# Another order of the expert passes in the two mixture-of-experts stages

## The chip, the cores and the metric

One core of one Trainium2 chip runs the whole kernel. The metric is the device time of one execution in microseconds (us). The times below are those of whole executions; the rows come from one profiled execution of the same program.

## What is computed

Two blocks of two layers each act on 256 tokens of width 1024, all in fp32. The first block alternates a token mixer with a mixture of experts (MoE): in each of its two layers a router gives every token two of 16 experts, out of one group of four, and an expert is a gated pair of products. The second block (attention and a dense MLP) is not touched by the change. Of the reference, this is the part at issue:

```python
logits = h2 @ router_w; scores = sigmoid(logits)
...
def run_block(args):
    tok, g, e = args
    xb = h2[tok]
    y = (silu(xb @ w1[e]) * (xb @ w3[e])) @ w2[e]
    return y * g[:, None]
```

Each expert has w1 and w3 (1024 x 512) and w2 (512 x 1024), 2 MB (of 1,048,576 bytes) each in fp32: 6 MB an expert, 96 MB a layer, and every expert's weights are read once per layer.

## The kernel before

**Ranks and passes.** The router counts the tokens of each expert and ranks the experts by that count, rank 0 having the most. Lists of ranks, not of experts, are fixed in the program: `PASSES` (line 23) holds seven passes. A pass of one expert uses all 128 columns of TensorE's array for up to 128 tokens; a pass of two gives each expert 64 columns, a pass of four gives each 32. Which ranks share a pass sets how many tokens a rank may have (`CAPS`, line 25); tokens beyond that go through `overflow` (line 797), a branch that stands between the last two passes and that is passed over here. `GROUPS` (line 24) names the passes, by their place in the order, that are prepared together.

**Loads.** Weights come in loads of 1 MB each, half of a matrix, on SP's queue in exactly the order of `sources()`: the up loads of pass p, then the down loads (w2) of pass p-1. A load of rank r needs that rank's expert number in a register of SP (line 889). The loads land in nine buffers in turn (`KINDS["wide"]`), so load k+9 can be issued only when the matmuls of load k are done. Each layer has 96 loads; they are numbered 1 to 96 here.

```python
def sources():
    up = lambda p: [(A[w], r, j) for w in ("w1", "w3") for j in range(2) for r in PASSES[p]]
    down = lambda p: [(A["w2"], r, j) for j in range(2) for r in PASSES[p]]
    for p in range(NP + 1):
        yield from up(p) if p < NP else ()
        yield from down(p - 1) if p else ()
```

**Matmuls.** `tiles` (line 954) takes the loads of one matrix half of a pass together, here called a group: one load in a pass of one expert, two or four otherwise. Its 4 products for each expert are issued in turn over the experts, whose columns of the array work side by side, and the first matmul of a group waits until all its loads have landed (line 963). A pass has four groups up (`up_`: two of w1, two of w3) and two groups down (`down`).

**Order of the work on TensorE.** `prep(g)` (line 916) gathers the tokens of the passes of one group of `GROUPS` with one-hot matmuls (lines 933 to 944). `up_(p)` ends with SiLU, a product and four transposes (line 976). `combine` (line 993) adds two finished passes into xT (lines 1000, 1002). The loop over p runs up_(p), down(p-1), after every second pass combine, and prep of the next group, two passes ahead:

```python
for p in range(NP + 1):
    if p < NP:
        at[p] = up_(p, pr[p])
    if p:
        todo.append((pr[p - 1][1], down(p - 1, at.pop(p - 1))))
        if len(todo) == 2 or p == NP:
            combine(todo)
...
    if groups and GROUPS[groups[0]][0] == p + 2:
        pr.update(prep(groups.pop(0)))
    if p == NP - 2:
        fetch(KINDS["wide"][0])
```

The Tile framework may move single instructions of an engine past each other where no data forbids it; the queue of loads keeps the order above.

Of the kernel before, what the change touches and what calls it, by code (L numbers as in the profile page):

```python
# [19 lines left out]
S = 256  # L20
D = 1024
NE = 16
PASSES = [[8, 9, 10, 11], [0], [2, 3], [4, 5], [1], [6, 7], [12, 13, 14, 15]]
GROUPS = [[0, 1], [2, 3], [4, 5], [6]]
CAPS = [128 // len(p) for _, p in sorted((r, p) for p in PASSES for r in p)]
ALPHA = 4.0 ** 0.25
# [175 lines left out]
def body(tc, A, out, co, po):  # L202
# [3 lines left out]
    with ExitStack() as ctx:  # L206
# [654 lines left out]
        def moe(l):  # L861
# [30 lines left out]
# [7 lines that stand above are left out]
            def fetch(n):  # L899

                while len(ahead) < n:
                    w, r, j = next(todo_w, (None, 0, 0))
                    if w is None:
                        break
                    ahead.append((load(w[l][expert(r), j].rearrange("o p a n -> p (o a n)"), None, 2048), landing[0]))

            def taken(p):
                n = len(PASSES[p])
                fetch(n)
                return [ahead.pop(0) for _ in range(n)]  # L910

            NP = len(PASSES)
            todo_w = sources()
            wide = lambda p: 128 // len(PASSES[p])

# [701 lines left out]
```

## Time and profile before

| | |
|---|---|
| median of 3 runs | 1955.6 us (1955.56 to 1958.34) |
| the profiled execution's own time | 1955.22 us |
| its span, first to last instruction | 1953.4 us |
| mean granted TensorE clock | 0.959 of 2.4 GHz |
| first MoE layer: first load issued, last group of matmuls begun | 202.7 us, 457.55 us |
| second MoE layer: first load issued, last group of matmuls begun | 606.1 us, 858.35 us |

The time of an execution lies 1.8 us over its span. The two MoE layers take a quarter of the span between them. Busy time is a share of the whole span, over stages with different limits; the rows of a stage tell more.

### The profile page before, as it was taken

To read this page: it belongs to the slowest core of one execution; us is meant where nothing else is said; L and a number is where in the kernel's file an instruction comes from. 1 tells how busy PE (TensorE), PEld (TensorE's weight loads), DVE (VectorE), ACT (ScalarE), POOL (GpSimd) and SP (SyncE) were. 2 spreads that over 40 slices of the span, in tenths; PEclk is the share of its full clock that TensorE was granted. 3 is DMA by queue.
4 is the path that set the end of the run, shared out by engine and by line. 5 is a ranking of instruction groups with operands and counts; after the bars stand their busy time and mean duration, and the time that the engine had idled before them with its cause. 6 is when DMAs were issued, how large, how long until landed. Compare 5 with 4: busy or idle time off the path is not lost. (4 is left out here: it accounts for less than half of the span.)

```text
span 1953.4 us, 29087 instructions
## 1 busy us (share of the span) xinstructions
PE 1758.2 (90%) x11198; PEld 1256.4 (64%) x11198; DVE 1078.6 (55%) x2298; ACT 741.2 (38%) x1461; POOL 70.7 (4%) x88
## 2 busy tenths in 40 slices
PE   5999689967897799689999999999999999989997
PEld 4866234414783344237655779888888786669996
DVE  4987212104654112048778367678855767666665
ACT  3556100003642000124767355232323656544443
POOL 0000000000200000000010001000000200010000
PEclk8999899978998999889999999999999999989999
DMA  9685999997649999984100675555543220245551
GB/s 378 242 285 193 382 413 419 371 381 311 242 164 369 417 423 380 386 343 156 35 21 33 218 253 188 176 172 187 188 129 130 97 93 22 76 153 182 183 184 44
DMA packets 94361, 440.46 MB, mean 225 GB/s; under 512 B 10240, under 2 KB 10368, under 8 KB 69376
## 3 DMA queue, kind: packets, MB, share of 16 engines
q1 hardware_dynamic: 94208, 438.44, 60.0%
q8 instruction: 93, 1.52, 0.3%
q14 instruction: 60, 0.49, 0.1%
HBM read 437.35 MB, written 1.05 MB: 224 GB/s over the span
## 5 line engine op out<-in xcount | busy, mean ns | idle before, releaser
L332 ACT CAST wh<-raw 128x1024 fp32r<-128x1024 f32 (+1 forms) x258 | 261.4, 1016 | 281.8 <-PE psL L346 209.8
L325 DVE TENSOR_TENSOR wl<-raw,wh 128x1024 fp32r<-128x1024 f32 (+1 forms) x258 | 305.3, 1185 | 97.8 <-ACT wh L332 97.4
L959 PE MATMUL psab<-raw,xg 128*32 128x512 f32 (+2 forms) x1024 | 226.2, 705 | 76.1 <-DMA raw<-w 62.8
L344 PE MATMUL psL<-h,wh 128*128 128x256 f32 (+1 forms) x800 | 258.4, 323 | 7.6 <-ACT h L340 7.6
L345 PE MATMUL psL<-h,wl 128*128 128x256 f32 (+1 forms) x800 | 257.8, 323 | 4.0 <-DVE wl L325 3.9
L346 PE MATMUL psL<-h,wh 128*128 128x256 f32 (+1 forms) x800 | 256.4, 321 | 0.0
L959 PEld LDWEIGHTS psab<-raw,xg 128*32 128x32 f32 (+2 forms) x1024 | 73.9, 147 | 221.7 <-issue 193.7
L344 PE MATMUL psL<-gh,wh 128*128 128x256 f32 (+1 forms) x576 | 185.1, 322 | 0.0
L345 PE MATMUL psL<-gh,wl 128*128 128x256 f32 (+1 forms) x576 | 184.6, 321 | 0.0
L344 PEld LDWEIGHTS psL<-h,wh 128*128 128x128 f32 x800 | 154.2, 193 | 23.4 <-ACT h L340 8.3
L973 DVE SCALAR_TENSOR_TENSOR sa<-sa,gs,psab 128x512 f32<-128x512 f32 x14 | 10.5, 747 | 282.5 <-PE psab L959 282.5
L345 PEld LDWEIGHTS psL<-h,wl 128*128 128x128 f32 x800 | 154.2, 193 | 18.5 <-DVE wl L325 5.1
L346 PEld LDWEIGHTS psL<-h,wh 128*128 128x128 f32 x800 | 153.9, 193 | 14.2 <-issue 4.2
L959 PE MATMUL psY<-raw,at 128*32 128x512 f32 (+2 forms) x512 | 113.1, 611 | 9.3 <-DMA raw<-w 8.4
L346 PE MATMUL psL<-o,wh 128*128 128x256 f32 (+1 forms) x384 | 119.3, 311 | 0.3
L344 PEld LDWEIGHTS psL<-gh,wh 128*128 128x128 f32 x576 | 109.5, 190 | 14.5 <-issue 5.8
L345 PEld LDWEIGHTS psL<-gh,wl 128*128 128x128 f32 x576 | 109.5, 190 | 11.1 <-issue 3.7
L340 ACT CAST yh<-psY 128x512 fp32r<-128x512 f32 x28 | 16.4, 586 | 245.5 <-PE psY L959 245.5
L346 PE MATMUL psL<-gl,wh 128*128 128x256 f32 (+1 forms) x288 | 91.9, 319 | 0.0
L1525 ACT ACTIVATE t<-psL 128x256 f32<-128x256 f32 (+1 forms) x72 | 32.8, 456 | 139.1 <-PE psL L346 139.1
L1123 DVE SCALAR_TENSOR_TENSOR xT<-psL,mod2T,xT 128x256 f32<-128x256 f32 x80 | 38.6, 483 | 84.2 <-PE psL L346 84.0
L344 PE MATMUL psL<-hh,wh 128*128 128x256 f32 x256 | 77.8, 305 | 7.0 <-ACT hh L518 5.5
(449 smaller groups left out, 3340.9 us busy)
## 6 DMA issues: line engine op xcount, KB each, us to landing
raw<-w SPq DMA_DIRECT2D x192, 1024.0 KB, 11.7
raw<-fc SPq DMA_DIRECT2D x144, 512.0 KB, 3.5
raw<-mod_w SPq DMA_DIRECT2D x80, 512.0 KB, 6.6
raw<-w_mod SPq DMA_DIRECT2D x80, 512.0 KB, 3.9
raw<-wo SPq DMA_DIRECT2D x24, 512.0 KB, 4.7
raw<-wi SPq DMA_DIRECT2D x18, 512.0 KB, 3.3
raw<-ev_in SPq DMA_DIRECT2D x16, 512.0 KB, 7.4
raw<-mod_w SPq DMA_DIRECT2D x8, 1024.0 KB, 10.3
```

What stands on the lines that cost most here:

```text
L325: eng.tensor_sub(o, a, hi)
L332: SC.copy(hi[:, :w], raw[:, :w])
L340: SC.copy(hi, src)
L344: T.matmul(o, lhsT=wh, rhs=xh, start=start, stop=False)
L345: T.matmul(o, lhsT=wl, rhs=xh, start=False, stop=False)
L346: T.matmul(o, lhsT=wh, rhs=xl, start=False, stop=stop)
L959: r = T.matmul(o[w * i:w * i + w, :], lhsT=x[:, w * i:w * i + w], rhs=loads[i][0][:, c:c + 512], start=first, stop=last)
L973: V.scalar_tensor_tensor(sa, sa, gs, ob, op0=OP.mult, op1=OP.mult)
L1123: V.scalar_tensor_tensor(src2[s][:, n, :], o[:, s * S:s * S + S], mod2T[l][:, g, s, n:n + 1], src2[s][:, n, :], op0=OP.mult, op1=OP.add)
L1525: SC.activation(t[:, a:b], o[:, a:b], AF.Relu)
```

## The change

One line: the order in which the seven passes run. The lists within the passes stay, and with them the capacities; `GROUPS` stays and so joins other passes: prep(0) still serves ranks 0 and 8 to 11, prep(1) now serves ranks 1, 2, 3, and prep(2) ranks 4 to 7. The last two passes stay where they are.

```diff
-PASSES = [[8, 9, 10, 11], [0], [2, 3], [4, 5], [1], [6, 7], [12, 13, 14, 15]]
+PASSES = [[0], [8, 9, 10, 11], [1], [2, 3], [4, 5], [6, 7], [12, 13, 14, 15]]
 GROUPS = [[0, 1], [2, 3], [4, 5], [6]]
```

Loads and groups in the order of SP's queue, "4 x 1" being four groups of one load; u is up, d is down:

| | before | after |
|---|---|---|
| loads 1 to 20 | u 4 x 4, u 4 x 1 | u 4 x 1, u 4 x 4 |
| loads 21 to 38 | d 2 x 4, u 4 x 2, d 2 x 1 | d 2 x 1, u 4 x 1, d 2 x 4, u 2 x 2 (of 4 x 2) |
| loads 39 to 58 | u 4 x 2, d 2 x 2, u 4 x 1, d 2 x 2 | u 2 x 2, d 2 x 1, u 4 x 2, d 2 x 2, u 1 x 2 (of 4 x 2) |
| loads 59 to 68 | u 4 x 2, d 2 x 1 | u 3 x 2, d 2 x 2 |
| loads 69 to 96 | u 4 x 4, d 2 x 2, d 2 x 4 | the same |

## Rows read from the trace of the kernel before

**Rows 1.** The page: busy engines, and 40 slices of DMA rates.
```profile
PE 1758.2 (90%) x11198; PEld 1256.4 (64%) x11198; DVE 1078.6 (55%) x2298; ACT 741.2 (38%) x1461; POOL 70.7 (4%) x88
...
GB/s 378 242 285 193 382 413 419 371 381 311 242 164 369 417 423 380 386 343 156 35 21 33 218 253 188 176 172 187 188 129 130 97 93 22 76 153 182 183 184 44
```

**Rows 2.** TensorE's timeline, end of the first MoE layer: start, duration, work, [idle].
```profile
457.55 5.34 PE L959 MATMUL psY<-raw,at 128*32 128x512 f32 x26 [1.39 <-DMA raw<-w]
```

**Rows 3.** First layer, stretches: busy by engine, granted clock, DMA share, GB/s.
```profile
270.00:280.00 10.00, 9.03 (x71) 3.15 (x69) 1.69 (x3) 0.60 (x2) 0.00 (x0) 1.00 0.95 369
...
340.00:350.00 10.00, 10.00 (x26) 4.29 (x23) 1.38 (x2) 1.61 (x3) 0.00 (x0) 1.00 1.02 428
370.00:380.00 10.00, 10.00 (x61) 5.27 (x62) 1.01 (x3) 1.00 (x3) 0.00 (x0) 1.00 0.55 203
380.00:390.00 10.00, 10.00 (x43) 3.84 (x40) 1.44 (x2) 0.55 (x1) 0.00 (x0) 1.00 0.96 392
400.00:410.00 10.00, 8.86 (x60) 2.76 (x64) 0.00 (x0) 1.48 (x2) 0.00 (x0) 0.67 0.55 209
```

**Rows 4.** The same stretches of the second layer.
```profile
680.00:690.00 10.00, 7.17 (x41) 2.40 (x32) 1.38 (x2) 1.17 (x2) 0.00 (x0) 0.83 0.98 392
770.00:780.00 10.00, 10.00 (x70) 6.75 (x71) 2.95 (x8) 0.96 (x2) 0.00 (x0) 1.00 0.58 220
780.00:790.00 10.00, 10.00 (x45) 3.38 (x42) 0.75 (x1) 0.60 (x1) 0.00 (x0) 1.00 0.95 398
800.00:810.00 10.00, 7.06 (x52) 2.14 (x56) 0.00 (x0) 1.47 (x2) 0.00 (x0) 0.70 0.61 235
```

**Rows 5.** SP's queue: loads 68 and 78 issued, each with its time to landing.
```profile
L321 SPq DMA_DIRECT2D raw<-w x1: 333/333/333, 376.5 to 376.5; - x1
...
DMA to landing us min/median/max: 7.4/7.4/7.4
...
L321 SPq DMA_DIRECT2D raw<-w x1: 333/333/333, 407.5 to 407.5; - x1
...
DMA to landing us min/median/max: 4.7/4.7/4.7
```

**Rows 6.** TensorE's timeline, first layer, later: passes of two, combine, the branch.
```profile
308.48 0.68 PE L1000 MATMUL psX<-PT,yh 128*128 128x256 f32 x1
...
318.04 13.95 PE L959 MATMUL psab<-raw,xg 128*64 128x512 f32 x64
...
340.59 14.00 PE L959 MATMUL psab<-raw,xg 128*128 128x512 f32 x32
...
401.14 9.80 PE L959 MATMUL psab<-raw,xg 128*32 128x512 f32 x64 [6.89 <-DVEq L804]
```

**Rows 7.** TensorE's timeline, first layer, passes [8, 9, 10, 11] and [0].
```profile
214.51 0.50 PE L944 MATMUL psX<-rt,P 128*128 128x1 f32 x4
217.00 3.64 PE L959 MATMUL psab<-raw,xg 128*32 128x512 f32 x32 [1.98 <-DMA raw<-w]
226.70 6.54 PE L959 MATMUL psab<-raw,xg 128*32 128x512 f32 x32 [6.07 <-DMA raw<-w]
...
246.24 7.23 PE L959 MATMUL psab<-raw,xg 128*32 128x512 f32 x36 [4.67 <-DMA raw<-w]
253.31 0.60 PE L976 MATMUL psX<-cst,sa 128*128 128x128 f32 x4
...
258.78 12.26 PE L959 MATMUL psab<-raw,xg 128*128 128x512 f32 x28
271.96 0.65 PE L976 MATMUL psX<-cst,sa 128*128 128x128 f32 x4 [0.92 <-DVE sa L973]
```

**Rows 8.** TensorE's timeline, start of the second layer's passes.
```profile
619.26 0.50 PE L944 MATMUL psX<-rt,P 128*128 128x1 f32 x4
619.70 3.64 PE L959 MATMUL psab<-raw,xg 128*32 128x512 f32 x32
629.58 6.49 PE L959 MATMUL psab<-raw,xg 128*32 128x512 f32 x32 [6.24 <-DMA raw<-w]
```

## The prediction

> **What bounds the kernel now.** I read the page first. TensorE is busy for 90% of the span, but in the slices of the two MoE layers (the fifth to the tenth and the thirteenth to the eighteenth) the DMA engines move 370 to 420 GB/s, more than anywhere else [rows 1]. So in these stages the loads are to be looked at, not the busy share. The timeline at the end of a layer says it plainly: the last group starts at 457.55, when its loads land, with TensorE idle before it [rows 2]. What comes after (5.3 us of matmuls, combine, the next norm) hangs on that moment alone, so a change is worth what it moves the landing of load 96 in each layer.
>
> Next I read the layers in stretches of 10 us. Where the queue is full it moves 428 GB/s [rows 3], which is 1,048,576 bytes / 428 GB/s = 2.45 us a load. The reader is to look for stretches with less: there SP held no free buffer. What a stretch lost is 10 x (1 - rate/428). The first layer lost 1.4 at 270, 5.3 and 0.8 at 370 and 380, and 5.1 at 400: 12.6 us [rows 3]. The second lost the same three holes: 0.8 at 680, 4.9 and 0.7 at 770 and 780, 4.5 at 800: 10.9 us [rows 4]. Together 23.5 us of DMA time.
>
> The holes of 370 and 400 are those of loads 68 and 78: each was issued late, at 376.5 and 407.5, and landed 7.4 and 4.7 us later [rows 5]. Both waited for a buffer. In the timeline TensorE works without idle time before load 68: passes of two and the lone pass [1] take 14.0 us each, whether a group is one load or two [rows 6]. A group costs 14.0 / 4 = 3.5 us; at full rate DMA brings one, two or four loads in 2.45, 4.9 or 9.8 us. A lone pass is thus slower than DMA (3.5 against 2.45 a load), the others faster. TensorE waits early, on [8, 9, 10, 11]: 6.07 and 4.67 us shown, a third such wait between them [rows 7]; then it runs late, and nine buffers do not span the lateness.
>
> **The change, step by step.** Its matmuls, loads, bytes and instructions are the same in number; only places change. Loads 69 to 96 come in the same order. The register loads of expert numbers move: four loads of one expert come first and need one number instead of four. That is at most a microsecond or two, and nothing hangs on it, since the first group can't start before prep(0) is done: taken as 0.
>
> *Start.* prep(0) ends at 214.51 + 0.50 = 215.0 [rows 7] and at 619.7 in the second layer [rows 8]. Before, TensorE then waited for four loads, until 217.0. Now load 1 is enough. Four lone groups take 4 x 3.5 = 14.0: to 229.0 and 633.7. Their buffers come back one by one, long before DMA has brought the nine loads that it holds.
>
> *The new hole, at load 14.* Next in the program stand the transposes and prep(1): from 253.31 to 258.78 before, 5.5 us [rows 7], with 0.92 ahead of the transposes for `sa`, as at 271.96 [rows 7], and 0.2 of slack: 6.6. So the first group of [8, 9, 10, 11] starts at 235.6 and takes 3.64, as the group of 217.0 [rows 7]: its four buffers come back at 239.2 (second layer: 643.9), and load 14 is issued 0.1 later. By then the queue is empty: load 13 is due at 217.0 + 9 x 2.45 = 239.05; in the second layer load 8 lands at 629.58 [rows 8] and load 13 at 641.8. A load issued to an empty queue lands after 4.7 to 7.4 us [rows 5]; I take the mean, 6.05. Load 14 lands at 245.35 instead of 241.5, hole 3.85, and at 650.05 instead of 644.25, hole 5.8. Sum 9.7; 7.0 at the shorter end, 12.4 at the longer.
>
> The Trainium skill (DMA: Bandwidth & Descriptors, Anatomy of one DMA) puts a transfer at a fixed 2.0 us plus bytes over 436 GB/s, fitted on another issue path: an estimate of 4.4 us for 1 MB. The row of load 78, 4.7, is near it; that of load 68 is not, as other loads followed at once and shared the engines. By the page the new holes would sum to 6.4 and the time would be 1939.1.
>
> *After load 14.* I count from load 20, which TensorE waits for (260.05 in the first layer: 245.35 + 6 x 2.45). Its group, after a wait, takes 5.5 (7.23 less four records of the next lone group [rows 7]); transposes 1.5 (0.92 and 0.65 [rows 7]), six lone groups 21.0, transposes 1.5, the first down group of four 3.5: 33.0. Load 36 is issued then and lands at 39.05 after load 20; due are 16 x 2.45 = 39.2. No hole, barely; with 6.5 for the first group, as the one at 226.70 had [rows 7], 0.85.
>
> From load 34 (294.35) TensorE has 3.5 left of that pass, combine and prep(2) 9.6 (308.48 to 318.04 [rows 6]), 14.0, 1.5, 7.0, 14.0, 1.5, 7.0, again at most 9.6: it begins up of [6, 7] at 362.0. Load 59's group ends at 369.0; load 68 lands at 375.05, and is due at 245.35 + 54 x 2.45 = 377.65. The hole of load 68 goes: lone pass [1] no longer stands in this stretch.
>
> TensorE ends the pass before the branch at 362.0 + 14.0 + 1.5 + 7.0 = 384.5 and starts again 6.9 later [rows 6], at 391.4; a group of 3.5 to 6.5 us; load 78 lands at 400.95 to 403.95, due 402.15. Hole 0 to 1.8, where there were 5.1. For this and load 36 I take 0.5 a layer, bounds 0 and 2.65. The second layer runs through the same sum from its load 20.
>
> *Sum.* Old holes 23.5, less new ones 9.7, less 1.0: 12.8 us sooner. The profiled execution took 1955.2 (span 1953.4 and 1.8 around it), 0.4 under the median: 1955.2 - 12.8 = 1942.4. Ends: 23.5 - 7.0 - 0 = 16.5 (1938.7), and 23.5 - 12.4 - 5.3 = 5.8 (1949.4).
>
> **Rivals.** *prep(1) is not in the way.* The order on TensorE isn't strictly the program's: four records of the next pass went ahead of the transposes (36 records at 246.24, then 28 [rows 7]). If prep(1) runs in the wait for load 16 instead, the first group of four ends at 229.0 + 1.5 + 3.65 = 234.1, load 14 lands at 240.2, before it is due; in the second layer at 644.9, 0.6 late. Gain 23.5 - 0.6 - 1.0 = 21.9: 1933.3. Against it: prep(1) came before the bulk of the next pass in this trace.
>
> *The hole moves to load 36.* Six lone groups stand in a row there and the margin is 0.15. If TensorE is 6.4 us later a layer at that point than I sum, as two of the six groups at half the clock would make it, the gain is gone: 1955.2; from 4 us on it is mostly gone. For it: groups behind waits took 6.54 and 6.49 instead of 3.64 [rows 7, 8]. Against it: the lone groups behind the wait of 246.24 ran 28 records in 12.26 us, full speed [rows 7].
>
> *Slower: the first lone groups run at 1.2 GHz.* They stand where load 14 depends on them. At 6.5 instead of 3.5, four of them bring load 14 12 us later in each layer: 1942.4 + 24 = 1966.4. It decides from 3.5 + 12.8/8 = 5.1 us a group on. For it: the group at 629.58 took 6.49 [rows 8]. The Trainium skill (TensorE: Matmul & The Clock Gate, HAM oscillation) tells of groups that start cold after each wait for DMA; the rows behind waits agree. Against it: the first group of each layer took 3.64, right behind prep(0) [rows 7, 8], and the lone groups would stand in that very place.
>
> **How the numbers follow.** The forecast (8 to 19 us gained) 0.58; more, through prep(1) or short landings, 0.14; 4 to 8, a part of the margin lost, 0.10; within 3.9 us (0.2%, about what a measurement here can tell from nothing), through load 36, 0.09; slower 0.09. Faster 0.82. The likeliest: 1942.4, own range 1938.7 to 1949.4. For 8 in 10 the range takes in most of the second and third case: 1933 to 1951.
>
> **What would show it.** In the profile after, rates stay at 420 GB/s or more from load 20 to the end of a layer: no stretch near 203 or 220. One new stretch falls short shortly after 239 and 644, by 3 to 6 us. TensorE's first four groups have 8 records each of 3.5 us, start at 215, and prep(1) follows. It waits for loads 16 and 20. The branch ends near 391 instead of 401, and the last group starts near 448 instead of 457.55. The prediction is wrong if the first lone groups take over 5 us, if load 14 is issued much before or after 239, or if the rate breaks in at load 36 or 78.

## The result, and the profile after

| | before | after |
|---|---|---|
| median of 4 runs each | 1956.97 us | 1942.94 us (1940.48 to 1943.91) |
| the profiled execution, its span | 1955.22, 1953.4 us | 1940.48, 1938.7 us |

The ratio of the two is 0.9913 with a 95% interval from 0.9896 to 0.9930: 0.7 to 1.0% faster. Forecast were 1942.4 us and a gain of 12.8; the profiled executions differ by 14.7, the medians by 14.0.

Stretches of the kernel after, first layer and second (columns as in [rows 3]); where they repeat those of [rows 3] and [rows 4], DMA now runs at or near its full rate, and one new place in each layer, two stretches long, does not:

```profile
230.00:240.00 10.00, 9.79 (x88) 6.92 (x92) 3.75 (x16) 1.89 (x4) 0.00 (x0) 1.00 0.59 249
240.00:250.00 10.00, 3.55 (x32) 0.85 (x28) 0.00 (x0) 0.60 (x1) 0.00 (x0) 0.89 0.96 381
...
290.00:300.00 10.00, 9.72 (x77) 3.60 (x70) 1.86 (x4) 1.17 (x2) 0.00 (x0) 1.00 1.01 422
...
370.00:380.00 10.00, 9.05 (x44) 3.15 (x42) 1.44 (x2) 0.00 (x0) 0.00 (x0) 1.00 1.01 424
380.00:390.00 10.00, 3.04 (x18) 1.19 (x18) 1.38 (x2) 2.69 (x5) 0.00 (x0) 0.89 1.01 421
...
400.00:410.00 10.00, 5.49 (x40) 1.38 (x35) 0.00 (x0) 0.60 (x1) 0.00 (x0) 0.84 1.01 426
...
620.00:630.00 10.00, 9.08 (x66) 6.77 (x68) 3.77 (x13) 1.89 (x4) 0.00 (x0) 1.00 0.94 399
630.00:640.00 10.00, 6.02 (x59) 1.56 (x48) 0.57 (x5) 0.60 (x1) 0.00 (x0) 1.00 0.64 251
...
770.00:780.00 10.00, 6.11 (x30) 2.10 (x26) 1.38 (x2) 2.45 (x3) 0.00 (x0) 1.00 1.02 428
...
800.00:810.00 10.00, 5.08 (x32) 1.31 (x32) 0.00 (x0) 0.00 (x0) 0.00 (x0) 0.79 1.02 430
```

Lost at 428 GB/s, reckoned as in the prediction: 4.2 and 1.1 us at 230 and 240, 0.7 and 4.1 at 620 and 630, together 10.1 (forecast for load 14: 9.7). The stretches of 370, 380 and 400, which lost 11.2 us of the first layer before [rows 3], lose 0.3; those of 770 and 800 in the second, which lost 9.4 [rows 4], lose nothing.

TensorE's timeline after, first layer (columns as in [rows 2]). The reader is to see the four lone groups at the front (32 records, eight to a group), without a wait among them; transposes and prep(1) to 235.8; two groups of [8, 9, 10, 11] back to back, whose loads had long landed; then the waits for loads 16 and 20:

```profile
214.95 0.51 PE L944 MATMUL psX<-rt,P 128*128 128x4 f32 x4
215.31 13.98 PE L959 MATMUL psab<-raw,xg 128*128 128x512 f32 x32
230.21 0.66 PE L976 MATMUL psX<-cst,sa 128*128 128x128 f32 x4 [0.92 <-DVE sa L973]
...
235.82 7.07 PE L959 MATMUL psab<-raw,xg 128*32 128x512 f32 x64
249.34 6.29 PE L959 MATMUL psab<-raw,xg 128*32 128x512 f32 x32 [6.45 <-DMA raw<-w]
259.25 6.45 PE L959 MATMUL psab<-raw,xg 128*32 128x512 f32 x32 [3.62 <-DMA raw<-w]
...
389.81 6.02 PE L959 MATMUL psab<-raw,xg 128*32 128x512 f32 x32 [6.96 <-DVEq L804]
...
447.88 3.64 PE L959 MATMUL psY<-raw,at 128*32 128x512 f32 x26 [1.39 <-DMA raw<-w]
```

The last group starts at 447.88, before 457.55 [rows 2]. In the second layer it starts 17 us sooner than the 858.35 of before, but its 26 records take 5.52 us where the same records took 3.64 before; the first line is of the kernel before, the second of the kernel after:

```profile
858.35 3.64 PE L959 MATMUL psY<-raw,at 128*32 128x512 f32 x26 [1.41 <-DMA raw<-w]
...
841.38 5.52 PE L959 MATMUL psY<-raw,at 128*32 128x512 f32 x26 [0.52 <-DMA raw<-w]
```

SP's queue of loads after: load 13 of the first layer, load 14 of both layers, and load 78 of the first.

```profile
L321 SPq DMA_DIRECT2D raw<-w x1: 332/332/332, 229.3 to 229.3; - x1
...
DMA to landing us min/median/max: 8.4/8.4/8.4
...
L321 SPq DMA_DIRECT2D raw<-w x1: 333/333/333, 239.5 to 239.5; - x1
...
DMA to landing us min/median/max: 4.9/4.9/4.9
...
L321 SPq DMA_DIRECT2D raw<-w x1: 333/333/333, 632.6 to 632.6; - x1
...
DMA to landing us min/median/max: 4.7/4.7/4.7
...
L321 SPq DMA_DIRECT2D raw<-w x1: 332/332/332, 395.8 to 395.8; - x1
...
DMA to landing us min/median/max: 7.0/7.0/7.0
```

### The profile page after: what moved, and what is told of

It reads as the page before. It is cut to its first block, busy times and chain, and to the rows that moved or that the text cites. A ratio compares the mean times of both kernels' runs of the same rounds, so it can differ in the third digit from the quotient of the medians.

```text
span 1938.7 us, 29085 instructions
## 1 busy us (share of the span) xinstructions
PE 1757.4 (91%) x11198; PEld 1255.2 (65%) x11198; DVE 1078.4 (56%) x2298; ACT 741.2 (38%) x1461; POOL 69.3 (4%) x88
## 5 line engine op out<-in xcount | busy, mean ns | idle before, releaser
L959 PE MATMUL psab<-raw,xg 128*32 128x512 f32 (+2 forms) x1024 | 220.2, 691 | 60.4 <-DMA raw<-w 46.6
L344 PEld LDWEIGHTS psL<-h,wh 128*128 128x128 f32 x800 | 154.6, 193 | 23.5 <-ACT h L340 8.3
L340 ACT CAST yh<-psY 128x512 fp32r<-128x512 f32 x28 | 16.4, 585 | 273.9 <-PE psY L959 273.9
L1123 DVE SCALAR_TENSOR_TENSOR xT<-psL,mod2T,xT 128x256 f32<-128x256 f32 x80 | 38.7, 483 | 84.2 <-PE psL L346 83.9
L959 PEld LDWEIGHTS psY<-raw,at 128*32 128x32 f32 (+2 forms) x512 | 35.9, 132 | 75.9 <-issue 59.2
## 6 DMA issues: line engine op xcount, KB each, us to landing
raw<-w SPq DMA_DIRECT2D x192, 1024.0 KB, 12.8
```

The lines of the kernel that those rows point to most:

```text
L344: T.matmul(o, lhsT=wh, rhs=xh, start=start, stop=False)
L959: r = T.matmul(o[w * i:w * i + w, :], lhsT=x[:, w * i:w * i + w], rhs=loads[i][0][:, c:c + 512], start=first, stop=last)
L1123: V.scalar_tensor_tensor(src2[s][:, n, :], o[:, s * S:s * S + S], mod2T[l][:, g, s, n:n + 1], src2[s][:, n, :], op0=OP.mult, op1=OP.add)
```

## The experiments

The theory under test: in both layers time is lost only where DMA has no free buffer, so the time follows from the sum of these holes, wherever they stand. A hole is what a stretch moved less than 428 GB/s, put as time. Rivals were that the gain comes from the earlier start (one landed load instead of four), that TensorE's work merely moves, and that early lone passes are good in themselves. Each kernel was timed in five rounds beside the kernel before, whose medians were 1958.69 us with the first four kernels and 1960.86 with the second four; ratios are to those. Medians of different rounds can differ by as much as those of the kernel before do (1956.97, 1958.69, 1960.86), so kernels of different rounds are best compared by their ratios.

**Half of the change: [0] to the front.**

```diff
-PASSES = [[8, 9, 10, 11], [0], [2, 3], [4, 5], [1], [6, 7], [12, 13, 14, 15]]
+PASSES = [[0], [8, 9, 10, 11], [2, 3], [4, 5], [1], [6, 7], [12, 13, 14, 15]]
```

> Half of the change alone: pass [0] goes to the front, pass [1] stays fifth. Theory of the buffers (time is lost only where DMA has no free buffer): the hole near load 14 appears (about 4 us a layer), the one at load 30 (about 2 us) goes, and those at loads 68 and 78 stay, since the lone pass [1] still stands between the passes of two. Net -1 to +3 us against the kernel before: 1954 to 1958. Rival, the early start (the gain comes from beginning each layer on one landed load instead of four): nearly the whole gain, 1941 to 1945.

Measured: 1961.81 us, ratio 1.0015 (1.0003 to 1.0028). The early start alone gains nothing: it is 3.1 us slower by the medians, at the slow end of what was expected (-1 to +3). Stretches of its first layer, columns as before:

```profile
230.00:240.00 10.00, 9.08 (x74) 6.50 (x75) 4.34 (x16) 1.89 (x4) 0.00 (x0) 1.00 0.76 320
240.00:250.00 10.00, 4.89 (x48) 1.29 (x40) 0.00 (x0) 0.60 (x1) 0.00 (x0) 0.85 0.74 294
270.00:280.00 10.00, 10.00 (x39) 3.64 (x39) 1.38 (x2) 1.17 (x2) 0.00 (x0) 1.00 1.01 425
370.00:380.00 10.00, 10.00 (x63) 5.71 (x64) 1.48 (x5) 0.96 (x2) 0.00 (x0) 1.00 0.77 301
...
400.00:410.00 10.00, 7.95 (x52) 2.40 (x56) 0.00 (x0) 1.47 (x2) 0.00 (x0) 0.63 0.53 206
```

The new hole is there (2.5 and 3.1 us), the one at 270 is gone, and those of 370 and 400 stay (3.0 and 5.2 us, where they were 5.3 and 5.1): the new one is paid and little is bought with it. That the early start by itself makes the gain is ruled out.

**The other half: [1] from fifth to third.**

```diff
+PASSES = [[8, 9, 10, 11], [0], [1], [2, 3], [4, 5], [6, 7], [12, 13, 14, 15]]
```

> The other half alone: [8, 9, 10, 11] stays first, pass [1] moves up to third. Theory of the buffers: load 30 stays late (2 us), eight lone groups in a row make a new hole at load 44 (4 to 5 us), load 68 is on time and load 78 late by 1 to 2 instead of 5. About 5.5 us a layer gained: 1942 to 1946. Rival, the early start: no gain, 1953 to 1957.

Measured: 1945.12 us, ratio 0.9937 (0.9915 to 0.9960). Most of the gain is here, perhaps all of it: the interval overlaps that of the change (0.9896 to 0.9930), so it is not shown that moving [0] to the front adds anything to moving [1].

```profile
270.00:280.00 10.00, 9.08 (x73) 2.96 (x72) 1.74 (x3) 0.58 (x1) 0.00 (x0) 1.00 0.90 361
310.00:320.00 10.00, 10.00 (x48) 3.48 (x49) 0.63 (x4) 1.01 (x3) 0.00 (x0) 1.00 0.77 303
370.00:380.00 10.00, 9.05 (x44) 3.06 (x42) 1.44 (x2) 0.60 (x1) 0.00 (x0) 1.00 1.01 424
400.00:410.00 10.00, 3.76 (x36) 1.18 (x32) 0.00 (x0) 0.60 (x1) 0.00 (x0) 0.84 1.00 419
```

The holes of 370 and 400 go when no lone pass stands between the passes of two, the one at 270 stays, and the two lone passes one behind the other open a new one at 310 (2.9 us, load 44; 4 to 5 were expected).

**prep(1) held back into the wait for load 16.** The order of the change, but the matmuls of prep(1) may stand on TensorE only behind the second group of [8, 9, 10, 11]; an order on the same engine, no new wait.

```diff
-            def prep(g):
+            def prep(g, behind=None):
+                def put(r):
+                    if behind:
+                        tc.add_manual_dep(r.ins, behind, nosync, reason="prep in the wait")
...
-            def up_(p, pr):
+            def up_(p, pr, between=None):
...
                 for o in (oa, ob):
+                    if o is ob and between:
+                        between()
...
-                    at[p] = up_(p, pr[p])
+                    at[p] = up_(p, pr[p], (lambda: pr.update(prep(groups.pop(0), last_mm[0]))) if p == 1 else None)
```

> The changed kernel with prep(1) held back on TensorE until the second group of [8, 9, 10, 11], that is into the wait for load 16. Theory of the buffers: load 14 is issued 5 us earlier, its hole (4.2 and 4.7 us) goes, and prep(1) costs nothing where it stands: 8 to 9 us under the changed kernel, 1932 to 1936. Rival (the hole only moves on, to load 36, since TensorE's work is the same in sum): within 2 us of the changed kernel.

Measured: 1933.63 us, ratio 0.9868 (0.9849 to 0.9886), which lies below the interval of the changed kernel: it beats both. Its timeline, first layer (line 937 is prep, line 965 the groups):

```profile
230.43 3.64 PE L965 MATMUL psab<-raw,xg 128*32 128x512 f32 x32
235.19 3.64 PE L965 MATMUL psab<-raw,xg 128*32 128x512 f32 x32 [1.12 <-DMA raw<-w]
238.76 0.50 PE L937 MATMUL psX<-P,th 128*128 128x256 f32 x2
...
242.45 0.41 PE L937 MATMUL psX<-P,tl 128*128 128x256 f32 x2
244.98 3.64 PE L965 MATMUL psab<-raw,xg 128*32 128x512 f32 x32 [0.94 <-DMA raw<-w]
```

and its rates in the first layer, with no hole at load 14 and none that came in its place:

```profile
230.00:240.00 10.00, 8.88 (x78) 3.56 (x78) 0.69 (x1) 0.60 (x1) 0.00 (x0) 1.00 1.01 422
240.00:250.00 10.00, 7.68 (x68) 4.89 (x67) 2.90 (x14) 1.89 (x4) 0.00 (x0) 1.00 1.01 428
290.00:300.00 10.00, 9.89 (x80) 7.61 (x73) 5.96 (x12) 1.76 (x3) 0.00 (x0) 1.00 1.01 424
```

The first group of four now ends at 234.1, the time that the rival of the prediction had worked out for it, and load 14 is issued at 234.1 instead of 239.5. Moving prep(1), 5.5 us long, out of the front of this release was worth 9.3 us by the medians (8.8 by the ratios), that is some 4.5 us a layer: most of its length, and in the wait it cost nothing that these rows show.

**prep(1) one pass later.**

```diff
-                if groups and GROUPS[groups[0]][0] == p + 2:
+                if groups and GROUPS[groups[0]][0] == p + (1 if groups[0] == 1 else 2):
```

> The changed kernel with prep(1) one pass later: after the whole of up of [8, 9, 10, 11] and the down groups of [0]. Theory of the buffers: load 14 is on time, but prep(1) now stands in the row of six lone groups, where the margin of load 36 was near 0: a hole of 4 us at loads 34 to 36 takes the place of the one at load 14. No change against the changed kernel, 1940 to 1945. If the hole at load 14 were only a matter of the place of prep(1) and margins elsewhere were wide, 8 us less.

Measured: 1939.98 us, ratio 0.9906 (0.9887 to 0.9925); the changed kernel had 0.9913 (0.9896 to 0.9930). The hole went from 230 to 290:

```profile
230.00:240.00 10.00, 7.34 (x65) 2.46 (x68) 1.44 (x2) 0.00 (x0) 0.00 (x0) 1.00 1.01 427
280.00:290.00 10.00, 10.00 (x27) 4.03 (x25) 0.75 (x1) 0.60 (x1) 0.00 (x0) 1.00 0.99 408
290.00:300.00 10.00, 9.89 (x82) 4.26 (x81) 2.41 (x4) 1.17 (x2) 0.00 (x0) 1.00 0.88 341
```

0.5 and 2.0 us here, 1.8 in the second layer's stretch of 680 (352 GB/s), so somewhat less than the 4 expected; in time it can't be told from the change. That is the prediction's rival of the hole that moves to load 36, brought about by the edit.

**Eight buffers instead of nine**, in the kernel before, the changed one and the one with prep(1) in the wait; more than nine was not tried.

```diff
-        KINDS = {"long": (11, 1024, 4), "wide": (9, 2048, 0), "short": (6, 1024, 3)}
+        KINDS = {"long": (11, 1024, 4), "wide": (8, 2048, 0), "short": (6, 1024, 3)}
```

> The kernel before with eight buffers of 1 MB instead of nine. Theory of the buffers: each old hole grows (loads 27 to 29 by 2.5 us, load 47 by 2.5, load 67 stays at that of load 68 plus what DMA runs ahead), about 5 us a layer: 8 to 12 us over the kernel before in the same runs. Rival (the lost time is TensorE's own, not DMA's): no change.

> The changed kernel with eight buffers. Theory of the buffers: the hole of load 14 comes one load sooner and is 2.45 us longer, and a new one of 1.6 us opens at load 35: 4.4 us a layer, 7 to 11 us over the changed kernel: 1948 to 1953. It stays faster than the kernel before with nine. Rival: no change.

> prep(1) in the wait for load 16 (now with eight buffers). Theory of the buffers: holes of 1.3 us at load 13 and 1.6 at load 35, 3.2 to 3.8 us a layer: 6 to 8 us over the same kernel with nine buffers, 1939 to 1943, about as fast as the changed kernel with nine.

Measured: 1976.97 us (ratio 1.0094, 1.0070 to 1.0119), 1959.32 (1.0002, 0.9986 to 1.0018) and 1948.31 (0.9944, 0.9926 to 0.9961). Against the same kernels with nine buffers that is 16.1, 16.4 and 14.7 us more: the direction of the theory, in no case the size of the expectation (8 to 12, 7 to 11, 6 to 8). The changed kernel with eight was expected to stay faster than the kernel before with nine; it is no faster. Part of the difference lies ahead of the layers. Each layer begins with loads of the conditioning weights in the same buffers, which I had left out: the first load of an expert is issued at 205.9 in the changed kernel with eight, at 202.1 with nine. And the hole at load 14, now load 13, is 8.1 us long, not 5.3 + 2.45:

```profile
230.00:240.00 10.00, 9.08 (x57) 6.82 (x55) 2.82 (x4) 1.52 (x3) 0.00 (x0) 1.00 0.77 305
240.00:250.00 10.00, 7.10 (x65) 1.99 (x65) 1.52 (x12) 0.97 (x2) 0.00 (x0) 0.97 0.54 203
```

The rest is in further holes: from the first load issued to the last group begun, the two layers together take 11.4, 12.4 and 14.2 us longer with eight buffers than with nine, and the stretches under 428 GB/s account for 11.3, 12.4 and 13.5 of it (table below). In the changed kernel with eight, 2.3 us of it stand at 400 and 420 of the first layer (371 and 385 GB/s), where no hole was expected.

**Another order altogether.**

```diff
+PASSES = [[2, 3], [4, 5], [0], [6, 7], [8, 9, 10, 11], [1], [12, 13, 14, 15]]
```

> A wholly different order with nine buffers and prep where the program puts it: [2, 3], [4, 5], [0], [6, 7], [8, 9, 10, 11], [1], [12, 13, 14, 15]. Each lone pass stands between passes of two or four, so that TensorE never falls far behind. Theory of the buffers: no hole at load 14, one of 2.3 us at load 72: 1932 to 1938, near the kernel with prep(1) in the wait. If what counts is lone passes early, as in the changed kernel, it is slower than that one: 1945 or more.

Measured: 1944.7 us, ratio 0.9922 (0.9901 to 0.9944): as fast as the change, but 6.7 us over the upper end of the expectation. It lost more than summed:

```profile
290.00:300.00 10.00, 10.00 (x57) 4.60 (x57) 1.13 (x5) 1.93 (x4) 0.00 (x0) 1.00 0.84 332
...
370.00:380.00 10.00, 10.00 (x36) 4.08 (x38) 0.75 (x1) 0.60 (x1) 0.00 (x0) 1.00 0.98 375
380.00:390.00 10.00, 6.17 (x56) 1.80 (x56) 2.07 (x3) 2.45 (x3) 0.00 (x0) 1.00 0.87 331
```

A hole of 2.2 us at 290 that I had put at nothing, and 1.2 and 2.3 at 370 and 380 for one of 2.3: 3.4 us more in this layer, and 3.5 in the second, whose stretches of 690, 770 and 780 moved 333, 306 and 397 GB/s. So the miss is again in holes that were held to be just avoided, not in another place. The time by itself stands at the border of the rival (1945 or more); what speaks against it is that no lone pass is among the first two here and the time is that of the change all the same.

## Why the prediction was right

*What sets the end of a layer.* Shown: in both layers of all ten kernels the last group begins within 0.1 us of the landing of load 96. The table has, of each profiled execution, the holes (of both layers, every whole stretch of 10 us under 428 GB/s from 5 us after the first load's issue on), the two layers from first load issued to last group begun, and the median.

| kernel | holes, us | two layers, us | median, us |
|---|---|---|---|
| prep(1) in the wait | 3.3 | 481.9 | 1933.63 |
| prep(1) later | 7.3 | 486.2 | 1939.98 |
| the change | 12.4 | 491.4 | 1942.94 |
| another order altogether | 13.7 | 493.3 | 1944.70 |
| [1] alone moved | 13.6 | 492.6 | 1945.12 |
| prep(1) in the wait, 8 buffers | 16.8 | 496.1 | 1948.31 |
| before | 27.4 | 507.1 | 1956.97 |
| the change, 8 buffers | 24.8 | 503.8 | 1959.32 |
| [0] alone moved | 30.8 | 509.2 | 1961.81 |
| before, 8 buffers | 38.7 | 518.5 | 1976.97 |

Less their holes the layers take 478.4 to 479.8 us in all ten. As the bytes are the same, holes and layers must go together; what the table adds is that no layer's end waited for anything else, and that the medians rise in nearly the same order. That a hole comes from a missing buffer is shown by the issue times: load 14 after the change was issued at 239.5, within 0.1 us of the end of the group that gave its buffer back, when load 13 had landed at 237.7.

*The start.* Forecast 215.0 and 14.0 us for four lone groups; 215.31 and 13.98. The slower rival, lone groups at 1.2 GHz, did not come: the four took 13.98 us together, and the clock granted while they ran was 1.00 of 2.4 GHz:

```profile
220.00:230.00 10.00, 9.29 (x22) 3.80 (x20) 0.59 (x1) 0.60 (x1) 0.00 (x0) 1.00 1.01 428
```

*The hole at load 14.* prep(1) did stand in front: the first group of four started at 235.82 (forecast 235.6), load 14 was issued at 239.5 (239.3) in the first layer and, the second layer beginning 10.4 us sooner, at 632.6 (644.0 less 10.4 is 633.6). It landed 4.9 and 4.7 us later, not 6.05. Loads 15 and 16, issued behind it within 1.2 us, followed it at the full rate, and the group that waits for load 16 began at 249.34, where the sum had 245.35 + 2 x 2.45 = 250.25. The term was 9.7, the rates give 10.1. That they are so near is partly luck. In the first layer the time to landing was put 1.1 us too long and load 13 was put 1.3 us too late (due 239.05, landed 237.7), and in the length of the hole these nearly cancel. In the prediction's own terms, the landing of load 14 against one load's time behind load 13, the holes were 4.2 and 3.9 us, 8.1 for 9.7. The rest of the 10.1 shows behind load 14: load 22 of the first layer and load 18 of the second landed another 1.0 and 1.5 us late, which was in no step.

*The rival that prep(1) is not in the way* was false for the change and true of the kernel that made it so: 9.3 us less by the medians (8.8 by the ratios), for 9.1 in the prediction (1942.4 less 1933.3).

*Loads 36, 68 and 78.* Forecast no hole, no hole, and 0 to 1.8 us. The stretch of 290, load 36's, ran at 422 GB/s, that of 680 in the second layer at 415. This one was close: the group behind load 20 took 6.45 us and not 5.5, so that load 36 was issued 34.2 us after that group began and not 33.0, which by the sum makes a hole of about 0.8; the lateness of load 22 had put off by 1.0 what was due. The branch ended at 389.81 (391.4); load 78 was issued at 395.8 and landed 7.0 later at 402.8, due 402.15 by the forecast; the rate stayed at 426. All three held, load 36 by this luck, and the half for [1] alone shows that it is this lone pass that had made 68 and 78 late.

*The sum.* 23.5 - 10.1 = 13.4, and 14.7 between the profiled executions. The 23.5 left out smaller holes of the kernel before, the largest of them 0.9 us in the first layer:

```profile
320.00:330.00 10.00, 10.00 (x48) 3.31 (x46) 0.00 (x0) 0.60 (x1) 0.00 (x0) 1.00 0.97 388
```

With all of them (table) the holes shrank by 15.0 us, and the layers by 15.7. The first layer's last group came 9.7 us sooner, 0.6 of it from before the layer, for 8.25 forecast. The second layer's last group started another 6.6 sooner than its first load, for 4.6, but took 5.52 us instead of 3.64 (the 26 records of both), so 1.9 was given back. In the first layer it was the other way round: these records took 5.34 us before [rows 2] and 3.64 after, 1.7 gained. Neither term was in a step, and that they nearly cancel is luck.

*A slip without effect.* The slices named as those of the MoE layers move 311 to 423 GB/s, not 370 to 420, and the first slice of the page, with 378, is not below all of them [rows 1]. The argument goes by the stretches of 10 us and does not need this.

## What to carry to other kernels

Where a ring of buffers feeds two kinds of work, one slower and one faster than DMA, the order of the work was worth time here only through the moments when no buffer was free: list, for each load, when its buffer is given back and when the queue would otherwise run dry, and put the slow kind apart, so that its lateness never adds up over the ring's length. Side work (here a gather) that stands in front of a release for which DMA waits cost most of its length; the same work in a wait for a load was free, so look for such a place first, and check on the engine's own order that the scheduler left it there. A margin of 1 to 2 us in such a sum is not a margin: the expectations that missed here rested on holes held to be just avoided, and a step of the prediction that held (load 36) did so by luck.

## What the runs showed of the hardware that was not expected

In the ten traces sixteen loads of 1 MB were issued when every load before them had landed. Fourteen landed 4.7 to 4.9 us after their issue, one after 5.3, and load 68 of [rows 5] after 7.4. Load 68 of the second layer, in the same trace, took 4.7:

```profile
L321 SPq DMA_DIRECT2D raw<-w x1: 333/333/333, 778.7 to 778.7; - x1
...
DMA to landing us min/median/max: 4.7/4.7/4.7
```

In both layers the next load was issued 1.2 us behind it, and the other fifteen had followers as soon or sooner. So the prediction's reason for the 7.4, that other loads followed at once and shared the engines, does not set it apart; what does stays open, and the mean of 6.05 was a mis-sized term. The time that a hole loses by the rates is longer than this load's lateness (5.3 and 4.2 us in the first layer of the changed kernel).

The Trainium skill (DMA: Bandwidth & Descriptors, Anatomy of one DMA), whose figures gave an estimate of 4.4 us for one load, is near the landing of that one load. The 1939.1 us that the prediction drew from it is 3.8 below the median and 1.4 below the profiled execution; the holes by the rates sum to 10.1 us and not to 6.4.

TensorE's clock fell behind the long waits for loads. Behind a wait of 6.45 us the third group of four took 6.29 us at a granted clock of 0.57, near the lower of its two levels (1.2 of 2.4 GHz); with prep(1) in that wait TensorE was idle for 0.94 us, kept 1.00 and took 3.64. The first row is of the changed kernel, the second of the one with prep(1) in the wait:

```profile
249.34:255.63 6.29, 6.28 (x32) 1.39 (x32) 0.00 (x0) 0.00 (x0) 0.00 (x0) 0.57 1.02 430
...
244.98:248.60 3.62, 3.62 (x32) 0.94 (x32) 0.61 (x5) 0.00 (x0) 0.00 (x0) 1.00 1.01 425
```

The Trainium skill (TensorE: Matmul & The Clock Gate, HAM oscillation) describes groups that start cold behind waits for DMA, and these rows agree; filling the wait with other matmuls avoided it for this group. For the last groups of a layer the rows do not say what decides: in the first layer 26 records took 5.34 us before and 3.64 after, behind the same wait of 1.39 us.
